# Laying out the blocks of a triangular inverse with VectorE's 32x32 turns in place of transfers through DRAM

## The chip, the cores and the metric

The kernel runs on one core of a Trainium2 chip. The metric is device time in microseconds (us): the median over several runs, beside one more execution that was profiled.

The core's engines each work through their own instructions in program order: TensorE (PE, whose weight loads stand apart as PEld), VectorE (DVE), ScalarE (ACT), GpSimd (POOL) and SyncE (SP), which here issues almost all transfers. An instruction that waits holds up everything behind it on its engine.

## The reference

One step of a decoder layer for 256 prompt tokens and 8 x 8 sample tokens (320 in all, width 2048). A single projection `w_in` feeds two branches, a gated delta rule (32 heads of 128 x 128 state) and a sparse attention; both are projected, merged by gates and projected again. The change lies in the delta rule alone:

```python
a_strict = jnp.where(strict, einsum('bhnid,bhnjd->bhnij', kb, k) * decay, 0.0)
rhs = concatenate([v * beta[..., None], kb * exp(G)[..., None]], axis=-1)
sol = lax.linalg.triangular_solve(a_strict, rhs, left_side=True, lower=True, unit_diagonal=True)
```

The kernel solves this by forming the inverse of each unit triangular 128 x 128 matrix: its four 32 x 32 diagonal blocks are inverted first, and the rest follows from products of blocks.

## The kernel before

**The main stream.** `stream` walks over weight units of 1024 x 128 (512 KB). For each, SP loads `raw`, ACT rounds it to `whi`, DVE forms the rest `wlo = raw - whi`, and PE runs 24 matmuls of 128 x 320 (`xh` and `xl` by `whi`, `xh` by `wlo`). ACT's and DVE's share of a unit is emitted up to two units ahead of PE (`split_ahead`, `lead=2`), in three buffers each.

**Side work.** Everything else is written as generators (`kq_gen`, `inverse`, `prompt_chain`, `sample_chain`, `norm_gen` and others). After the sixth k of a unit and after its end, `side_round` lets each generator emit its next piece, if its inputs are ready by the planner's clock (`Clock`, which adds a price for every instruction). `spawn(..., first=True)` puts a generator ahead of the others. So the prices decide where in each engine's program a piece stands; on the chip only the order and the semaphores count.

**The recurrent stage** runs from about 850 us to 1660 us, in eight groups of four heads, one group for every 24 units of the stream. For a group, `kq_gen` forms twelve matrices in `BT` (128 x 12 x 128: four heads by two prompt chunks, and four for the samples). `inverse` turns them into `XT`, and `prompt_chain`, `sample_chain` and `norm_gen` go on from there. `norm_gen` sends a small power (`sc<-sc,mh`, 128 x 6) to POOL, and ACT's scaling of `ot` waits for it. There is one buffer each of `BT`, `blk`/`X` and `XT`.

**`inverse` before the change** (called from `kq_gen` once both head pairs of a group stand in `BT`):

1. Seven transfers write `BT`'s diagonal and off-diagonal blocks to DRAM (`d_b`, `d_o`); one reads the 48 diagonal blocks back into `blk`, one block to a partition.
2. POOL inverts all 48 together: 31 steps of a product (`tmpx`) and a subtraction (`X`), on 48 partitions.
3. POOL copies the result turned (`blk<-X`); two transfers write both forms to DRAM (`d_x`), and fifteen read blocks into `XT`, `blk` and `X` with rows on partitions.
4. PE multiplies blocks in four places: 16 products of 32 x 32 (`ps<-X,blk`), 28 more (`XT`, `blk`), 8 of 64 x 64 and 8 more. ACT brings each result from PSUM into `blk`, `X` or `XT`.

All transfers are issued by SP, in the queue that also carries the weights: 25 for a group, 200 in all.

## Time and profile before

| | |
|---|---|
| time, median of 3 runs (2125.87 to 2126.71) | 2125.89 us |
| time of the profiled execution | 2128.34 us |
| its span | 2126.6 us |
| granted TensorE clock | 0.998 |
| busy in the span: PE / DVE / ACT / POOL | 2093.1 / 1416.3 / 985.3 / 464.0 us |
| recurrent stage, 960 to 1660 us: PE / DVE / ACT / POOL | 698.4 / 522.1 / 396.8 / 313.4 us |

The span is the time from the first to the last instruction of the profiled execution; the launch around it adds 1.7 us. A row of the timeline has start, duration, engine, instruction, what it writes and reads, shapes and how many alike were merged; in brackets stands the idle time ahead of it and what ended it. All instructions are recorded by one helper, so they all carry one line number, and are told apart by the tiles that they write and read.

### The profile page before, as it was taken

The page shows a single profiled execution, that of the slowest core. Times are in us where ns is not written, and L with a number is a line of the kernel's source. Part 1 is how long each engine was busy: PE and PEld are TensorE (multiplying, and loading weights), DVE is VectorE, ACT ScalarE, POOL GpSimd, SP SyncE. Part 2 cuts the span into 40 slices and gives each one's busy share as a digit, 9 for nine tenths or more (in the row PEclk, how much of TensorE's full clock was granted, in tenths as well). Part 3 has the DMA queues.
Part 4 walks back from the last instruction along what each step waited for, and adds up shares of the span by engine and source line. Part 5 has one row for each costly group of instructions (what it writes and reads, how often), then busy time and mean ns, then how long its engine had stood idle before and what let it go on. Part 6 is the DMA issues. An engine that isn't in the chain of part 4 may idle for free.

```text
span 2126.6 us, 45305 instructions
## 1 busy us (share of the span) xinstructions
PE 2093.1 (98%) x17769; PEld 2020.2 (95%) x17769; DVE 1416.3 (67%) x2898; ACT 985.3 (46%) x2253; POOL 464.0 (22%) x661
## 2 busy tenths in 40 slices
PE   7999999999999999999999999999999999999997
PEld 7999989999999999899999999999999999999997
DVE  4776647889855477777878786868665545455543
ACT  3224473333344455465646464656545534333343
POOL 1001000000010108361818181818080000000000
PEclk9999999999999999999999999999999999999999
DMA  9996659776578667686868686868687867555562
GB/s 344 333 337 184 177 140 261 224 210 197 167 239 247 202 186 203 160 233 181 228 173 232 173 232 171 234 170 229 171 245 214 247 204 211 169 154 150 163 181 81
DMA packets 713989, 438.99 MB, mean 206 GB/s; under 512 B 73936, under 2 KB 697136, under 8 KB 711472
## 3 DMA queue, kind: packets, MB, share of 16 engines
q1 hardware_dynamic: 709696, 413.45, 68.3%
q0 software_dynamic: 3616, 21.02, 3.0%
q8 instruction: 139, 2.28, 0.5%
q10 hardware_dynamic: 464, 1.65, 0.2%
q14 instruction: 74, 0.61, 0.1%
HBM read 386.81 MB, written 48.94 MB: 205 GB/s over the span
## 4 chain that ended last, share of the span: by engine, by line
PE 70%; issue 22%; DVE 3%; DMA 2%; ACT 2%; SPq 0%; DVEq 0%; POOL 0%; POOLq 0%; ACTq 0%
PE pm L64 54%; PE ps L64 16%; DVE S L64 1%; DVE wlo L64 1%; DMA rawx<-in_w_ada_dram 1%; DMA a<-in_w_ada_dram 1%; DMA out_dram<-s 0%; DVE ps L64 0%; ACT whi L64 0%; DMA qiS<-d_qi 0%; ACT ot L64 0%; SPq L64 0%; DMA c<-in_c_sample_dram 0%; ACT s L64 0%; DMA cst<-in_state_conv_dram 0%
## 5 line engine op out<-in xcount | busy, mean ns | idle before, releaser
L64 PE MATMUL pm<-xh,whi 128*128 128x320 f32 (+1 forms) x3108 | 942.5, 317 | 2.7 <-DVE qiS L64 1.3
L64 PE MATMUL pm<-xl,whi 128*128 128x320 f32 (+1 forms) x3108 | 910.2, 307 | 0.3 <-DVE xl L64 0.2
L64 DVE TENSOR_TENSOR wlo<-raw,whi 128x1024 fp32r<-128x1024 f32 x466 | 576.8, 1247 | 245.8 <-ACT whi L64 233.7
L64 PEld LDWEIGHTS pm<-xh,whi 128*128 128x128 f32 x3108 | 584.2, 188 | 27.9 <-issue 20.2
L64 PEld LDWEIGHTS pm<-xl,whi 128*128 128x128 f32 x3108 | 585.0, 188 | 1.6 <-DVE xl L64 0.7
L64 ACT ACTIVATE whi<-raw 128x1024 fp32r<-128x1024 f32 x466 | 488.5, 1058 | 168.1 <-PE pm L64 103.8
L64 PE MATMUL pm<-xh,wlo 128*128 128x320 f32 (+1 forms) x3108 | 521.3, 307 | 0.5 <-DVE wlo L64 0.5
L64 PEld LDWEIGHTS pm<-xh,wlo 128*128 128x128 f32 x3108 | 469.4, 188 | 0.9 <-DVE wlo L64 0.9
L64 POOL TENSOR_TENSOR X<-X,tmpx 48x31 f32<-48x31 f32 (+15 forms) x248 | 175.5, 708 | 19.4
L64 POOL TENSOR_TENSOR tmpx<-blk,X 48x31 f32<-48x31 f32 (+15 forms) x248 | 162.0, 653 | 53.0 <-DMA blk<-d_b 34.8
L64 DVE SCALAR_TENSOR_TENSOR ps<-xp,cs,ps 128x344 f32<-128x344 f32 x192 | 111.5, 581 | 6.8
L64 POOL TENSOR_TENSOR sc<-sc,mh 128x6 f32<-128x6 f32 (+1 forms) x24 | 44.3, 1848 | 285.4 <-DVE sc L64 206.0
L64 PE MATMUL pm<-y1h,whi 128*128 128x320 f32 x336 | 99.5, 309 | 1.8 <-DVE M L64 0.9
L64 POOL TENSOR_TENSOR rfin<-rfin,mh 128x3 f32<-128x3 f32 x1 | 0.8, 848 | 455.5 <-DVE rfin L64 455.5
L64 PE MATMUL pm<-y1l,whi 128*128 128x320 f32 x336 | 99.1, 307 | 0.0
L64 DVE SCALAR_TENSOR_TENSOR S<-S,gtr,ps 128x128 f32<-128x128 f32 x256 | 67.4, 342 | 0.1
L64 PEld LDWEIGHTS pm<-y1h,whi 128*128 128x128 f32 x336 | 62.8, 187 | 2.3 <-ACT whi L64 2.3
L64 PE MATMUL ps<-xh,whi 128*128 128x320 f32 (+1 forms) x220 | 64.7, 309 | 0.0
L64 ACT ACTIVATE xp<-pm 128x256 f32<-128x256 f32 (+1 forms) x128 | 32.0, 304 | 70.5 <-PE pm L64 70.5
L64 ACT ACTIVATE ot<-ot,sc 128x128 f32<-128x128 f32 x96 | 29.9, 390 | 73.5 <-DVE sc L64 73.5
L64 PE MATMUL ps<-xl,whi 128*128 128x320 f32 (+1 forms) x220 | 63.7, 304 | 0.0
L64 PEld LDWEIGHTS pm<-y1l,whi 128*128 128x128 f32 x336 | 63.1, 188 | 0.0
(403 smaller groups left out, 2793.3 us busy)
## 6 DMA issues: line engine op xcount, KB each, us to landing
raw<-in_w_in_dram SPq DMA_DIRECT2D x328, 512.0 KB
raw<-in_w_pa_dram SPq DMA_DIRECT2D x64, 512.0 KB
rawx<-in_w_ada_dram SPq DMA_DIRECT2D x18, 1024.0 KB
a<-in_w_ada_dram SPq DMA_DIRECT2D x16, 1024.0 KB
S<-in_state_gdn_dram SPq DMA_DIRECT2D x32, 512.0 KB
out_dram<-S SPq DMA_DIRECT2D x32, 512.0 KB
raw<-in_w_pb_dram SPq DMA_DIRECT2D x32, 512.0 KB
raw<-in_w_out_dram SPq DMA_DIRECT2D x32, 512.0 KB
```

What stands on the lines that cost most here:

```text
L64: made = fn(*args, **kw)
```

## The change

The blocks stay in SBUF. ACT and POOL copy the 48 diagonal blocks of `BT` side by side into `X` (block k of a matrix stays on partitions 32k to 32k+31), and one DVE instruction turns all 32 x 32 squares, so that each partition holds one whole block; 80 of the 128 partitions then carry filler. POOL's 31 steps are the same with 128 partitions. Two more DVE turns bring the inverse back in both forms, and ACT and POOL copy blocks into place. The off-diagonal blocks go by copies into two new tiles, `BO` and `BD`. All 25 transfers of a group and their DRAM tiles are gone. `inverse` is spawned ahead of the other side work.

To make room, the mask is built a second time in `gdn_open` (`select`) instead of being kept, and the tiles `sc` shrink from 56 to 44 columns by letting `qf` and one of the tail factors use columns that are free by then.

```diff
-        self.tmp = a.tile([48, 256], F32, name="tmpx")
+        self.tmp = a.tile([128, 256], F32, name="tmpx")
+        self.BO = a.tile([128, 4, 64], F32, name="BO")
+        self.BD = a.tile([128, 8, 32], F32, name="BD")
...
-            self.spawn(self.inverse(h // 2, G))
+            self.spawn(self.inverse(h // 2, G), first=True)
...
+    def blocks(self, out, in_):
+        self.emitted += 1
+        self.nc.vector.transpose(out, in_)
...
-        for k in range(4):
-            nc.sync.dma_start(d_b[k].rearrange("m j i -> j m i"), BT[32 * k:32 * k + 32, :, 32 * k:32 * k + 32])
-        nc.sync.dma_start(d_o[:, :, 0:64], BT[0:64, 0:8, 64:128])
+        stage = X.rearrange("p (m i) -> p m i", i=32)
+        nc.gpsimd.memset(X[:, 384:1024], 0.0)
+        for k, s in enumerate(quarters):
+            if k % 2:
+                self.act(stage[s, 0:12, :], BT[s, :, s])
+            else:
+                nc.gpsimd.tensor_copy(stage[s, 0:12, :], BT[s, :, s])
+        BO, BD = self.BO, self.BD
+        self.act(BO[64:128], BT[0:64, 4:8, 64:128])
         for o in (0, 64):
-            nc.sync.dma_start(d_o[o // 2:o // 2 + 32, :, 64:96], BT[o:o + 32, 0:8, o + 32:o + 64])
+            self.act(BD[o:o + 32], BT[o:o + 32, 0:8, o + 32:o + 64])
+        nc.gpsimd.tensor_copy(BO[0:64], BT[0:64, 0:4, 64:128])
         self.BT.put(BT)
+        yield self.ready(X)
+        self.blocks(blk.rearrange("p (j i) -> p i j", i=32), X.rearrange("p (m i) -> p i m", i=32))
+        nc.gpsimd.memset(X, 0.0)
+        nc.gpsimd.memset(X[:, 0:1024:33], 1.0)
         yield
...
-        nc.gpsimd.tensor_copy(blk[0:48].rearrange("p (c i) -> p c i", i=32), X.rearrange("p i c -> p c i"))
         yield
...
-        nc.sync.dma_start(d_x[0].rearrange("k m i c -> (k m) (i c)"), Xt[0:48])
-        nc.sync.dma_start(d_x[1].rearrange("k m i c -> (k m) (i c)"), blk[0:48])
...
+        self.blocks(blk.rearrange("p (m i) -> p i m", i=32), X.rearrange("p (i c) -> p i c", c=32))
+        cols = X.rearrange("p (i c) -> p c i", c=32)
+        self.blocks(cols, cols)
...
+        for k, s in enumerate(quarters):
+            if k % 2:
+                self.act(XT[s, :, s], DT[s])
+            else:
+                nc.gpsimd.tensor_copy(XT[s, :, s], DT[s])
...
+        for o in (0, 32):
+            self.act(XE[o + 64:o + 96, :, o:o + 32], DN[o:o + 32, 4:8, :])
+            self.act(XE[o:o + 32, :, o:o + 32], DT[o + 64:o + 96, 4:8, :])
```

Three places in the program show what moves. The first is **POOL**, between the last step of one group's inverse and the first step of the next (`sc` of 128 x 10 belongs to `kq_gen`, of 128 x 6 to `norm_gen`). Before:

```order
L64 TENSOR_TENSOR X<-X,tmpx 48x31
L64 COPY blk<-X 48x1024
L64 TENSOR_TENSOR sc_8004<-sc_8004,mh 128x10
L64 MEMSET X 32x8x32
L64 MEMSET X 32x4x32 x2
L64 MEMSET X 48x1024
L64 MEMSET X 48x32
L64 TENSOR_TENSOR sc_8002<-sc_8002,mh 128x6
L64 TENSOR_TENSOR tmpx<-blk,X 48x31
```

And in the changed kernel, between two groups:

```order
L64 TENSOR_TENSOR X<-X,tmpx 128x31
L64 MEMSET X 32x4x32 x3
L64 COPY X<-X 32x4x32 x2
L64 COPY XT_7982<-blk 32x12x32 x2
L64 TENSOR_TENSOR sc_7999<-sc_7999,mh 128x10
L64 TENSOR_TENSOR sc_7998<-sc_7998,mh 128x6
L64 MEMSET X 128x640
L64 COPY X<-BT_7973 32x384 x2
L64 COPY BO<-BT_7973 64x256
L64 MEMSET X 128x1024
L64 MEMSET X 128x32
L64 TENSOR_TENSOR sc_8001<-sc_8001,mh 128x6
```

The turned copy is gone; seven copies, with a memset of 640 columns, have come, and the power of one `norm_gen` now stands behind them, and behind a memset of `X` that has to wait for DVE's first turn.

The second is **DVE**, where the two turns behind POOL's last step stand among the weights' `wlo`, in the changed kernel:

```order
L64 TENSOR_TENSOR wlo_82<-raw_75,whi_79 128x1024
L64 TENSOR_SCALAR sc_7998<-sc_7998 128x10
L64 TENSOR_TENSOR wlo_83<-raw_75,whi_80 128x1024
L64 STREAM_TRANSPOSE blk<-X 128x32x32
L64 STREAM_TRANSPOSE X<-X 128x32x32
L64 SCALAR_TENSOR_TENSOR zf_7967<-cth_7948,zf_7967 128x320
L64 TENSOR_TENSOR wlo_81<-raw_76,whi_78 128x1024
```

Before, DVE had nothing of the inverse there; now the `wlo` behind the turns waits until POOL is through.

The third is **ACT**, where the products of blocks come back from PSUM. Before, two pieces with a `whi` between:

```order
L64 ACTIVATE blk<-ps_70 32x256 x2
L64 ACTIVATE whi_79<-raw_75 128x1024
L64 ACTIVATE X<-ps_72 32x4x32 x2
L64 ACTIVATE X<-ps_67 32x4x32
L64 ACTIVATE XT_7986<-ps_72 32x8x32 x2
L64 ACTIVATE whi_80<-raw_75 128x1024
```

In the changed kernel:

```order
L64 ACTIVATE whi_80<-raw_77 128x1024
L64 ACTIVATE XT_7982<-blk 32x12x32 x2
L64 ACTIVATE X<-ps_67 32x4x32 x2
L64 ACTIVATE X<-ps_69 32x4x32
L64 ACTIVATE XT_7982<-ps_67 32x8x32 x2
L64 ACTIVATE X<-X 32x4x32
L64 ACTIVATE X<-blk 32x4x32
L64 ACTIVATE X<-X 32x4x32
L64 ACTIVATE X<-blk 32x4x32
L64 ACTIVATE whi_78<-raw_77 128x1024
```

Six copies have joined the five that were there, ahead of the same `whi`.

## The prediction

> **What bounds the kernel now.** I read the page's head first, then the busy time by stage, then single places.

> ```profile
> span 2126.6 us, 45305 instructions
> PE 2093.1 (98%) x17769; PEld 2020.2 (95%) x17769; DVE 1416.3 (67%) x2898; ACT 985.3 (46%) x2253; POOL 464.0 (22%) x661
> PE   7999999999999999999999999999999999999997
> ```

> PE is busy 98% of the span, and in all slices but the first and the last. The next view gives the three stretches that the change can reach: entry, body and what follows.

> ```profile
> 850.00:960.00 110.00, 107.96 (x880) 103.14 (x879) 82.37 (x198) 64.87 (x189) 55.08 (x78) 1.00 0.74 194
> 960.00:1660.00 700.00, 698.36 (x5755) 668.99 (x5755) 522.05 (x1230) 396.84 (x1076) 313.40 (x431) 1.00 0.75 204
> 1660.00:2115.00 455.00, 452.92 (x3105) 451.98 (x3103) 221.75 (x295) 169.65 (x250) 0.41 (x1) 1.00 0.59 172
> ```

> The columns after the length are PE, PEld, DVE, ACT, POOL, the granted clock, the DMA share and GB/s. PE stands idle for 2.04, 1.64 and 2.08 us in them: **5.8 us in all is what any change to the other engines could win here.** But a busy PE need not be at its peak, so its pace is looked at, in the timeline around one of the inverse's products:

> ```profile
> 1182.05 0.31 PE L64 MATMUL pm<-xh,whi 128*128 128x320 f32 x1
> 1182.20 0.30 PE L64 MATMUL pm<-xl,whi 128*128 128x320 f32 x1
> 1182.34 1.33 PE L64 MATMUL pm<-xh,wlo 128*128 128x320 f32 x8
> 1183.61 0.69 PE L64 MATMUL ps<-X,blk 32*32 32x32 f32 x32
> 1184.23 0.41 PE L64 MATMUL pm<-xh,whi 128*128 128x320 f32 x1
> 1184.48 0.30 PE L64 MATMUL pm<-xl,whi 128*128 128x320 f32 x1
> ...
> 1128.83 0.49 PE L64 MATMUL ps<-ident,ot 128*128 128x128 f32 x3
> 1129.08 0.39 PE L64 MATMUL pm<-xh,whi 128*128 128x320 f32 x1
> ```

> The main matmuls start every 0.147 us (1182.05, 1182.20, 1182.34), before and after a side product, and the 32 small ones follow within 0.1 us (eight from 1182.34 end their slots at 1183.52). So PE is issuing all the time; the inverse is inserted work, not something that PE waits for. In the waits of 960 to 1660 us there is indeed no row of PE for `blk`, `X` or `XT`; those that concern the stream's operands are:

> ```profile
> DVE wlo L64 <- ACT whi L64: 64.0, 38, 3.5
> ACT ot L64 <- DVE sc L64: 63.3, 13, 6.1
> ACT whi L64 <- PE pm L64: 13.0, 16, 1.9
> PEld pm L64 <- ACT whi L64: 2.8, 3, 1.2
> PE pm L64 <- ACT whi L64: 2.1, 3, 0.9
> ```

> No `whi` waits for a weight's transfer there. PE's few waits are for `whi`, and ACT's largest is for `sc`, which comes from POOL by way of DVE.

> **The change part by part.**

> *PE's work.* Each group keeps its products: 16 and 28 of 32 x 32, 8 and 8 of 64 x 64, with the same rows and columns of the array, only from other tiles. What differs is where they stand. Counted in the two programs, small work interrupts the stream at 323 places before and 311 after. Does an interruption cost something by itself? The three transposes above start at 1128.83 and the stream goes on at 1129.08, 0.25 us for three; the first main matmul of the other piece takes 0.25 us to the next instead of 0.147, and 0.09 us lay ahead. At the dearest 12 x 0.19 = 2.3 us are won, at the cheapest nothing, if these parts only begin and finish the small ones' own work, as the three transposes suggest. I take 0.

> *The transfers.* 200 leave SP's queue:

> ```profile
> DMA packets 713989, 438.99 MB, mean 206 GB/s; under 512 B 73936, under 2 KB 697136, under 8 KB 711472
> ```

> Most of the 73,936 small packets are theirs, rows of 32 numbers. Since `whi` doesn't wait for weights in this stage, this wins nothing: it is hidden already. What is late next is POOL.

> *What is added.* The prices come from these groups and single rows:

> ```profile
> L64 DVE STREAM_TRANSPOSE a<-a 128x1024 f32<-128x1024 f32 x24 | 28.6, 1222 | 0.0
> L64 POOL COPY blk<-X 48x1024 f32<-48x1024 f32 x8 | 18.7, 2336 | 0.5
> L64 POOL MEMSET X<- 48x1024 f32 x8 | 7.6, 952 | 148.8 <-PE ps L64 81.7 <-DMA d_z<-zf 44.8 <-DMA raw<-in_w_in_dram 22.4
> L64 POOL MEMSET XT<- 128x1536 f32 x1 | 1.4, 1385 | 0.5 <-DMA d_z<-t 0.5
> L64 POOL TENSOR_TENSOR X<-X,tmpx 48x31 f32<-48x31 f32 (+15 forms) x248 | 175.5, 708 | 19.4
> L64 POOL TENSOR_TENSOR tmpx<-blk,X 48x31 f32<-48x31 f32 (+15 forms) x248 | 162.0, 653 | 53.0 <-DMA blk<-d_b 34.8
> L64 ACT ACTIVATE xp<-pm 128x256 f32<-128x256 f32 x64 | 24.4, 381 | 70.5 <-PE pm L64 70.5
> L64 ACT ACTIVATE cth<-ps 128x344 f32<-128x344 f32 x64 | 29.0, 453 | 43.9 <-DVE ps L64 43.8
> L64 ACT ACTIVATE X<-ps 32x128 f32<-32x128 f32 x24 | 6.4, 268 | 5.6 <-PE ps L64 5.2
> ```

> - DVE: 3 turns of 1.22 us, 3.7 us for a group. That row reads along the columns, the new ones in steps of 128 bytes, which no DVE row shows. Bounds: 1.22 us, and 2.45 times that (3.0 us) by the ratio of POOL's turned copy to its memset (2336 to 952 ns). I take 1.22, the row of the same instruction.
> - ACT: four copies of 384 columns (0.48 each, between 0.381 and 0.453 and a little on), three of 256 (0.38), four of 128 (0.27): 1.92 + 1.14 + 1.08 = 4.1 us for a group.
> - POOL: copies at 0.93 to 2.28 ns a column (memset, turned copy), and I take the dearer: four of 384, one of 256, two of 128 make 2048 columns, 4.7 us; the memset of 640 adds 0.6 and the turned copy takes 2.3 away: 3.0 us more for a group.
> - The 31 steps cost 337.5 / 8 = 42.2 us for a group, on 48 partitions. With 128? From below the same: the memsets give 0.93 ns a column on 48 partitions and 0.90 on 128. From above 128/48 times, 112 us, if two-input steps went by partitions; no row shows one that wide. I take the same, because the only pair of rows says so.

> Over 107 us, a group's period (24 units), DVE goes from 75% to 78%, ACT from 57% to 61%, POOL from 45% to 48%. None is full, so on the average it is all beside PE.

> *Is the inverse in time?* In the changed order its first product stands at least 17 units (of 24 x 0.147 = 3.53 us) behind the last product that feeds `BT`, 60 us plus the small work between, some 65 us at the least. It needs six `BT` products on DVE (6 x 0.34), copies (2), a turn, the memset (1.0), 42.2 us with 62 gaps of 0.08 as the timeline shows them, and two turns: 2.1 + 2 + 1.2 + 1.0 + 47 + 2.4 = 56 us. With turns at 3.0 us it is 61, still in time. PE doesn't wait at the products.

> *Queues.* Where the two turns stand, all of DVE's later work waits for POOL's last step. But DVE prepares up to two units ahead, 7 us; a wait of some us there uses up lead, not PE's time. The tender place is another:

> ```profile
> 1121.08 1.87 ACT L64 ACTIVATE ot<-ot,sc 128x128 f32<-128x128 f32 x6 [5.37 <-DVE sc L64]
> 1127.84 1.99 ACT L64 ACTIVATE whi<-raw 128x1024 fp32r<-128x1024 f32 x2
> 1129.21 2.26 POOL L64 TENSOR_TENSOR sc<-sc,mh 128x6 f32<-128x6 f32 x1 [1.02 <-DVE sc L64]
> 1131.44 0.62 POOL L64 TENSOR_TENSOR tmpx<-blk,X 48x247 f32<-48x247 f32 x1
> ```

> ACT stood 5.37 us for `sc`, which had waited in POOL's queue behind steps of the inverse; afterwards it caught up, and of the pair of `whi` from 1127.84 the first was done near 1128.9, for a PE unit that starts at 1129.08. **The margin is about 0.2 us.** There are 16 such places, two for a group. The change moves POOL's chain against them, in each group otherwise. If a place becomes up to 1 us earlier or later, evenly, it loses on the mean (0.8 x 0.8 / 2) / 2 = 0.16 us beyond its 0.2 of margin: 16 x 0.16 = 2.6 us. Of PE's 2.1 us of waits for `whi` now, I let 0.5 go.

> [...] These rows show DVE and POOL in each other's way:

> ```profile
> 1134.33 0.62 POOL L64 TENSOR_TENSOR tmpx<-blk,X 48x255 f32<-48x255 f32 x1
> 1134.80 1.24 DVE L64 TENSOR_TENSOR wlo<-raw,whi 128x1024 fp32r<-128x1024 f32 x1
> 1135.03 1.55 POOL L64 TENSOR_TENSOR X<-X,tmpx 48x255 f32<-48x255 f32 x1
> ```

> The step at 1135.03 takes 1.55 us where most take 0.7: it stood until `wlo` was through. [...]

> **The sum.** PE's work 0, waits at the products 0, waits for `whi` +2.6 - 0.5 = +2.1 us. On the profiled execution that makes 2128.34 + 2.1; it stands 2.45 us above the median of the runs, so against the median 2125.89 + 2.1 = **2128.0 us**, within what a measurement can tell from no change (0.2%, 4.25 us).

> **The rivals.**

> 1. *Slower: the powers come late out of POOL.* The changed order puts memsets and copies, and in some groups DVE's first turn, ahead of `norm_gen`'s power. For it: 3.0 us more in that queue for a group, and margins of 0.2 us. Against it: the generators are paced, and chains now start earlier. It decides from 0.5 us of lateness at each of the 16 places on: 16 x 0.3 = 4.8 us, 2130.7; with 1 us, 16 x 0.8 = 12.8 us, 2138.7.
> 2. *Faster: the waits go.* Without transfers the chain starts earlier, and the powers may fall between chains. All 5.8 us of idle time gone gives 2120.1; under 2121.6 it counts as faster. Nearly every wait would have to vanish, though 2.1 us lie behind the stage.
> 3. *It doesn't do what it says:* the steps get dearer with the partitions, 112 us instead of 42.2, more than a group's period; the inverse would come some 60 us late in each group, about +500 us. The memsets speak against it.

> **Chances.** The forecast (within 4.25 us) 0.66; rival 1, 0.27; rival 2, 0.06; rival 3, 0.01. The range leaves out rival 3, rival 2's far end and the last of rival 1: 2121 to 2138. So faster by over 0.2% has 0.06, within it 0.66, slower 0.28.

> **What would show it.** Right: PE idle near 4 us over the three stretches, turns near 1.22 us, POOL's steps at the same mean, no PE wait for the inverse's tiles, DMA share lower in the stage with no effect on PE. Rival 1: rows of PE waiting for `whi` or `wlo` several times as large, each some us behind a late `sc`. Rival 3: steps of over 1 us at the mean. What would upset all this is a wait that no row shows now, above all DVE's turns holding a `wlo` for longer than its lead.

## The result and the profile after

| | before | after |
|---|---|---|
| median (range) | 2125.90 us (2125.87 to 2126.71) | 2155.39 us (2152.14 to 2156.28) |
| ratio, 95% interval | | 1.0135 (1.0117 to 1.0153) |
| profiled execution: time / span | 2128.34 / 2126.6 us | 2155.66 / 2154.0 us |
| mean granted clock | 0.998 | 0.994 |

The kernel became 29.5 us slower; 2128.0 had been forecast, with 2138 as the upper end. The head of the page of the changed kernel, and its packets:

```profile
span 2154.0 us, 45150 instructions
PE 2103.4 (98%) x17769; PEld 2026.9 (94%) x17769; DVE 1461.9 (68%) x2921; ACT 1023.8 (48%) x2341; POOL 492.9 (23%) x720
DMA packets 658436, 426.65 MB, mean 198 GB/s; under 512 B 19536, under 2 KB 642736, under 8 KB 655920
```

54,400 of the packets under 512 bytes are gone, PE runs as many matmuls, and its share of 98% looks as before. The same three stretches, columns as in the prediction:

```profile
850.00:960.00 110.00, 104.00 (x860) 97.68 (x859) 87.03 (x201) 63.34 (x183) 54.98 (x83) 0.98 0.58 160
960.00:1660.00 700.00, 685.62 (x5585) 654.72 (x5585) 546.51 (x1236) 418.55 (x1132) 333.46 (x471) 0.99 0.67 185
1660.00:2115.00 455.00, 453.90 (x3106) 453.50 (x3105) 226.39 (x301) 175.40 (x259) 1.32 (x1) 1.00 0.63 183
```

PE stands idle for 6.00, 14.38 and 1.10 us, 21.5 in all where it was 5.8. Behind the stage nothing is lost. In the first two stretches the granted clock is no longer 1.00. PE's largest waits from 850 to 1700 us (total, times, longest):

```profile
PE ps L64 <- DVE X L64: 8.9, 5, 2.9
PE pm L64 <- ACT whi L64: 6.1, 6, 1.5
PE pm L64 <- DVE wlo L64: 4.1, 5, 1.8
```

The first row is the wait that the prediction had ruled out: the inverse's first product (`ps<-X,BD`) waits for DVE's turn into `X`. The groups of the turns (busy, mean ns), the old ones of `a` for comparison:

```profile
L64 DVE STREAM_TRANSPOSE blk<-X 128x1024 f32<-128x1024 f32 x16 | 34.0, 2127 | 8.2 <-POOL X L64 8.2
L64 DVE STREAM_TRANSPOSE a<-a 128x1024 f32<-128x1024 f32 x24 | 28.6, 1223 | 0.0
L64 DVE STREAM_TRANSPOSE X<-X 128x1024 f32<-128x1024 f32 x8 | 17.0, 2121 | 0.3
```

The turns in steps of 128 bytes take 2.12 us, 1.74 times the contiguous one. What that does is seen in the timeline, first on DVE and then on PE, at the dearest place:

```profile
1505.08 2.00 DVE L64 STREAM_TRANSPOSE blk<-X 128x1024 f32<-128x1024 f32 x1 [3.01 <-POOL X L64]
1507.12 2.01 DVE L64 STREAM_TRANSPOSE X<-X 128x1024 f32<-128x1024 f32 x1
```

```profile
1509.27 0.74 PE L64 MATMUL ps<-X,BD 32*32 32x32 f32 x32 [2.92 <-DVE X L64]
1509.94 0.64 PE L64 MATMUL pm<-xh,whi 128*128 128x320 f32 x1
1510.37 0.47 PE L64 MATMUL pm<-xl,whi 128*128 128x320 f32 x1
1510.64 0.47 PE L64 MATMUL pm<-xh,whi 128*128 128x320 f32 x1
1510.91 0.47 PE L64 MATMUL pm<-xl,whi 128*128 128x320 f32 x1
```

PE waits 2.92 us, and afterwards the main matmuls start every 0.27 us (1510.37, 1510.64, 1510.91) in place of 0.147: for a while the clock is halved (granted clock 0.50 from 1509.79 to 1513.20 us). The clock's records put half clock into five slots of 3.41 us in the stage (from 854.4, 1025.1, 1175.3, 1509.8 and 1615.6 us), and into none there before the change. Windows cut along these slots show PE's busy time, then the granted clock:

```profile
851.02:854.43 3.41, 1.75 (x41) 1.00 0.00 0
854.43:857.85 3.42, 3.42 (x15) 0.50 0.61 168
1021.68:1025.10 3.42, 1.58 (x11) 1.00 0.39 109
1025.10:1028.51 3.41, 3.41 (x16) 0.50 0.83 213
...
1567.82:1571.23 3.41, 1.88 (x14) 1.00 1.00 265
1571.23:1574.64 3.41, 3.41 (x25) 1.00 0.76 205
```

The slots in which PE was busy for 1.75 and 1.58 us are followed by one at half clock; after 1.88 us the clock stays. At half clock a matmul takes 0.27 us (1510.37 to 1510.91 for two) in place of 0.147, so a slot costs 3.41 x (1 - 0.147 / 0.27) = 1.55 us, and five cost 7.8.

**Where the time went:** 15.7 us more idle time and 7.8 us at half clock make 23.5 of the span's 27.4 us; the other 4 us aren't placed.

### The profile page after: what moved, and what is told of

It is laid out like the page before. It is cut to its first block, busy times and chain, and to the rows that moved or that the text cites. A ratio compares the mean times of both kernels' runs of the same rounds, so it can differ in the third digit from the quotient of the medians.

```text
span 2154.0 us, 45150 instructions
## 1 busy us (share of the span) xinstructions
PE 2103.4 (98%) x17769; PEld 2026.9 (94%) x17769; DVE 1461.9 (68%) x2921; ACT 1023.8 (48%) x2341; POOL 492.9 (23%) x720
## 2 busy tenths in 40 slices
PE   7999999999999999999999999999999999999997
## 3 DMA queue, kind: packets, MB, share of 16 engines
q8 instruction: 139, 2.28, 0.4%
## 4 chain that ended last, share of the span: by engine, by line
PE 52%; issue 24%; DVE 9%; POOL 8%; DMA 3%; ACT 3%; SPq 1%; DVEq 0%; POOLq 0%; ACTq 0%
PE pm L64 38%; PE ps L64 14%; POOL X L64 4%; POOL tmpx L64 4%; DVE wlo L64 2%; DVE blk L64 1%; DVE S L64 1%; DVE ps L64 1%; DMA raw<-in_w_ada_dram 1%; SPq L64 1%; ACT whi L64 1%; ACT ot L64 1%; DMA rawx<-in_w_ada_dram 1%; DMA a<-in_w_ada_dram 1%; DVE X L64 0%
## 5 line engine op out<-in xcount | busy, mean ns | idle before, releaser
L64 PE MATMUL pm<-xh,whi 128*128 128x320 f32 (+1 forms) x3108 | 945.2, 318 | 8.1 <-ACT whi L64 6.1
L64 PE MATMUL pm<-xl,whi 128*128 128x320 f32 (+1 forms) x3108 | 913.4, 308 | 0.4 <-DVE xl L64 0.3
L64 DVE TENSOR_TENSOR wlo<-raw,whi 128x1024 fp32r<-128x1024 f32 x466 | 577.8, 1247 | 232.0 <-ACT whi L64 221.9
L64 PEld LDWEIGHTS pm<-xh,whi 128*128 128x128 f32 x3108 | 587.2, 189 | 33.8 <-issue 18.9
L64 PEld LDWEIGHTS pm<-xl,whi 128*128 128x128 f32 x3108 | 587.9, 189 | 1.6 <-DVE xl L64 0.8
L64 ACT ACTIVATE whi<-raw 128x1024 fp32r<-128x1024 f32 x466 | 489.4, 1058 | 178.9 <-PE pm L64 113.6
L64 PE MATMUL pm<-xh,wlo 128*128 128x320 f32 (+1 forms) x3108 | 524.7, 309 | 4.6 <-DVE wlo L64 4.6
L64 PEld LDWEIGHTS pm<-xh,wlo 128*128 128x128 f32 x3108 | 471.6, 189 | 6.9 <-DVE wlo L64 6.8
L64 POOL TENSOR_TENSOR X<-X,tmpx 128x31 f32<-128x31 f32 (+15 forms) x248 | 177.8, 717 | 19.4
L64 POOL TENSOR_TENSOR tmpx<-blk,X 128x31 f32<-128x31 f32 (+15 forms) x248 | 170.9, 689 | 18.6
L64 DVE SCALAR_TENSOR_TENSOR ps<-xp,cs,ps 128x344 f32<-128x344 f32 x192 | 111.5, 581 | 6.8
L64 POOL TENSOR_TENSOR rfin<-rfin,mh 128x3 f32<-128x3 f32 x1 | 0.8, 850 | 471.9 <-DVE rfin L64 471.9
L64 PE MATMUL pm<-y1h,whi 128*128 128x320 f32 x336 | 99.4, 308 | 0.0
L64 PE MATMUL pm<-y1l,whi 128*128 128x320 f32 x336 | 99.1, 307 | 0.0
L64 POOL TENSOR_TENSOR sc<-sc,mh 128x6 f32<-128x6 f32 (+1 forms) x24 | 41.3, 1719 | 236.4 <-DVE sc L64 164.4
L64 ACT ACTIVATE xp<-pm 128x256 f32<-128x256 f32 (+1 forms) x128 | 32.0, 304 | 76.0 <-PE pm L64 76.0
L64 DVE SCALAR_TENSOR_TENSOR S<-S,gtr,ps 128x128 f32<-128x128 f32 x256 | 67.5, 344 | 0.1
L64 PE MATMUL ps<-xh,whi 128*128 128x320 f32 (+1 forms) x220 | 64.7, 309 | 0.0
L64 ACT ACTIVATE ot<-ot,sc 128x128 f32<-128x128 f32 x96 | 29.9, 390 | 71.9 <-DVE sc L64 71.9
L64 PE MATMUL ps<-xl,whi 128*128 128x320 f32 (+1 forms) x220 | 63.7, 304 | 0.0
L64 PEld LDWEIGHTS pm<-y1l,whi 128*128 128x128 f32 x336 | 63.1, 188 | 0.0
L64 PEld LDWEIGHTS pm<-y1h,whi 128*128 128x128 f32 x336 | 62.8, 187 | 0.0
```

Of the source, the lines that this page charges most:

```text
L64: made = fn(*args, **kw)
```

## The experiments

My theory was: *the turns' steps make them long, the long turns come late for PE, and the longest of those waits halve the clock.* The rivals: *the place* (the planner's price of 1.245 us for a turn puts the products too early, and only that is wrong), and *the order* (any new order of the program, or late powers, whatever a turn takes). Results, in the order of the runs; each ratio is to the kernel before on the same chip, and the last column counts the slots at half clock in the profiled execution between 840 and 2120 us.

| kernel | median us | ratio (95%) | half-clock slots |
|---|---|---|---|
| changed kernel | 2155.39 | 1.0135 (1.0117 to 1.0153) | 5 |
| e1_flat: all turns contiguous | 2135.13 | 1.0038 (1.0025 to 1.0051) | 0 |
| e1_sides: first turn reads in steps only | 2155.07 (one run) | | 5 |
| e2_price: turn priced at 2.1 us | 2160.94 | 1.0164 (1.0138 to 1.0189) | 6 |
| e3_last: inverse spawned last | 2148.05 | 1.0095 (1.0076 to 1.0114) | 4 |
| e5_swap: product waits for one turn | 2137.79 | 1.0057 (1.0040 to 1.0074) | 1 |
| e6_t1: and the first turn contiguous | 2135.73 | 1.0043 (1.0026 to 1.0059) | 0 |
| e7_last: e6_t1, inverse last | 2135.69 | 1.0043 (1.0026 to 1.0059) | 1 |
| e8_norm: e7_last, scaling later | 2138.02 | 1.0063 (1.0046 to 1.0080) | 3 |
| e9_norm1: e6_t1, scaling later | 2136.59 | 1.0058 (1.0041 to 1.0075) | 1 |
| e10_norm: before, scaling later | 2134.71 | 1.0046 (1.0029 to 1.0063) | 2 |
| e4_first: before, inverse first | 2135.15 | 1.0051 (1.0032 to 1.0070) | 1 |
| e11_bpow: before, price of the power | 2128.11 | 1.0001 (0.9991 to 1.0010) | 0 |
| e12_bdve: before, price of DVE | 2133.65 | 1.0029 (1.0019 to 1.0038) | 0 |
| e13_spow: e6_t1, price of the power | 2139.87 | 1.0051 (1.0036 to 1.0066) | 2 |
| e14_sdve: e6_t1, price of DVE | 2147.25 | 1.0091 (1.0072 to 1.0110) | 1 |

### The turns' length alone

```diff
-        self.blocks(blk.rearrange("p (j i) -> p i j", i=32), X.rearrange("p (m i) -> p i m", i=32))
+        self.blocks(blk.rearrange("p (i c) -> p i c", c=32), X.rearrange("p (i c) -> p i c", c=32))
...
-        self.blocks(blk.rearrange("p (m i) -> p i m", i=32), X.rearrange("p (i c) -> p i c", c=32))
+        self.blocks(blk.rearrange("p (i c) -> p i c", c=32), X.rearrange("p (i c) -> p i c", c=32))
...
-        self.blocks(cols, cols)
+        self.blocks(X.rearrange("p (i c) -> p i c", c=32), X.rearrange("p (i c) -> p i c", c=32))
```

> The changed kernel with its three turns reading and writing along the columns (contiguous, as the turns of before did); every engine's order stays as in the changed kernel. It leaves out the right layout of the blocks, so the numbers in the inverse are others; the work is the same. Theory 1 (the turns are long because of their steps of 128 bytes, and come late for PE): a turn falls from 2.09 to about 1.25 us, PE's waits at the products (9.7 us) fall under 2, the half-clock windows go from five to none or one, and the time is 2132 to 2140 us. Theory 3 (the new order as such, the powers late out of POOL, whatever a turn takes): the products may come in time, but the whi and wlo waits stay (11 us) and with them some of the half-clock windows; 2146 or more.

This kernel leaves out the right layout of the blocks. The planner prices both forms alike, and on DVE, ACT and POOL the order of the rows in the trace is the changed kernel's, row by row. The groups of the turns, and PE's waits from 850 to 1700 us, in e1_flat:

```profile
L64 DVE STREAM_TRANSPOSE blk<-X 128x1024 f32<-128x1024 f32 x16 | 19.8, 1239 | 7.3 <-POOL X L64 7.3
L64 DVE STREAM_TRANSPOSE X<-X 128x1024 f32<-128x1024 f32 x8 | 10.0, 1246 | 0.3
```

```profile
PE pm L64 <- ACT whi L64: 6.0, 7, 1.3
PE ps L64 <- DVE X L64: 1.8, 2, 1.4
PE pm L64 <- DVE wlo L64: 1.3, 2, 0.9
```

0.88 us less for a turn takes 7.1 us from the product waits, 2.8 from `wlo`'s and every slot at half clock: 1.0135 falls to 1.0038. **About 20 of the 29 us are the turns' length**, shown with the order kept. The turns now also take what the planner prices (1.245 us), so this run doesn't part "long" from "longer than priced". The `whi` waits stay. Of the 8 us that e1_flat still loses, 7.4 are idle time of PE in the first two stretches (11.0 us against 3.7 before).

In e1_sides the first line alone is changed, to write contiguously while it reads in steps:

> The changed kernel with the first turn writing contiguously and still reading in steps of 128 bytes; the second writes in steps alone, the third reads and writes in steps, as they were. It leaves out the right layout. If the write's stride alone costs, the first turn takes about 1.25 us and the other two stay at 2.0 to 2.1; if the read's stride costs too, the first stays near 2.0. The time: under theory 1 somewhat below the changed kernel (one of a group's three turns shorter: 2148 to 2155), under theory 3 the same as the changed kernel.

These two rows of its timeline, at the places of two first turns:

```profile
886.46 1.96 DVE L64 STREAM_TRANSPOSE blk<-X 128x1024 f32<-128x1024 f32 x1
1021.83 2.03 DVE L64 STREAM_TRANSPOSE blk<-X 128x1024 f32<-128x1024 f32 x1
```

Reading in steps costs by itself nearly all (1.96 and 2.03 us); so does writing (the turn at 1505.08 above writes in steps and reads contiguously, 2.00). The time stayed that of the changed kernel, though it is a single run.

### The place of the products

```diff
+            if op == "transpose" and len(outs[0].shape) == 3:
+                return 2.1
```

> The changed kernel with its work untouched, but the planner's price of a turn in steps put at 2.1 us in place of 1.245, so that the products that wait for turns are emitted later. Theory 2 (only the place of the products in PE's order is at fault, since the planner took the turns too short): turns stay at 2.09 us, the product waits (9.7 us) fall under 3, the half-clock windows fall from five to one or two, 2136 to 2144 us. Theory 1 in its strict form (long turns hold DVE's queue and so wlo, wherever the products stand): wlo and whi waits stay at 11 us or grow; 2146 to 2152. Theory 3: 2150 or more.

PE's waits from 850 to 1700 us in e2_price, with the last row further down:

```profile
PE pm L64 <- ACT whi L64: 11.4, 8, 3.2
PE pm L64 <- DVE wlo L64: 8.0, 7, 1.8
...
PE ps L64 <- DVE X L64: 0.6, 1, 0.6
```

The products are now nearly in time, as that rival said, and yet the kernel is slower: `wlo` and `whi` wait longer. At 1135.19 us, for one, PE stands 1.84 us for a `wlo` that DVE could only begin behind a first turn of 2.16 us. The true price alone doesn't mend it: the turns are still long in DVE's queue, and the new order has bad places of its own. As "only the price is wrong" the rival falls. But the true price also moved the rows, and the order rival had asked for 2150 or more here, so this run doesn't say what late products cost by themselves; e5_swap says more of that.

### The first turn of two, and the turn ahead of `wlo`

e5_swap needs the right layout with fewer steps. The turn in steps now gives the form that the first product reads, and the other form is the contiguous turn of that:

```diff
-        self.blocks(blk.rearrange("p (m i) -> p i m", i=32), X.rearrange("p (i c) -> p i c", c=32))
-        cols = X.rearrange("p (i c) -> p c i", c=32)
-        self.blocks(cols, cols)
+        blk, X = X, blk
+        self.blocks(X.rearrange("p (m c) -> p c m", c=32), blk.rearrange("p (i c) -> p c i", c=32))
+        self.blocks(blk.rearrange("p (m i) -> p m i", i=32), X.rearrange("p (m c) -> p m c", c=32))
```

> The changed kernel, with the right layout, but the two turns behind the inverse rearranged: the one in steps of 128 bytes now gives the form that the first product reads, and the other form is made from it by a contiguous turn. So the first product waits for one turn of about 2.1 us and not for two (4.2 us), and the pair takes 3.3 us; the turn ahead of POOL's steps stays in steps. The order moves by a few rows only. If the long turns act through the products' lateness: the product waits (9.7 us) fall under 2, the half-clock windows behind them (four of five) go, the wlo waits (4.6 us) and the window at about 1025 us stay: 2155.4 - 9.7 - 4 x 1.7 = 2139, 2135 to 2143. If they act through DVE's queue alone (wlo held behind turns): one turn of a group shorter by 0.9 us, 2150 or more. If the order is at fault: 2150 or more.

PE's waits for these operands in e5_swap (the tiles' names are exchanged, so the product waits for `blk`):

```profile
PE pm L64 <- ACT whi L64: 5.0, 4, 1.5
PE pm L64 <- DVE wlo L64: 2.8, 3, 1.8
PE ps L64 <- DVE blk L64: 0.9, 1, 0.9
```

2137.8 against 2139: nearly all of the wait at the products goes, with its four slots, though two of a group's three turns are still long; the long `wlo` wait stays. So most of the turns' cost came through the late products. That the number fits so closely is in part luck: the half-clock slot at the `wlo` wait went too, and another came at 903 us. The windows along the slots show both:

```profile
1015.96:1019.38 3.42, 2.31 (x16) 2.05 (x14) 3.38 (x4) 2.90 (x8) 0.29 (x1) 1.00 0.77 223
1019.38:1022.79 3.41, 2.69 (x19) 2.68 (x20) 3.33 (x9) 1.06 (x1) 1.86 (x3) 1.00 0.40 108
899.91:903.32 3.41, 1.48 (x21) 0.83 (x14) 3.41 (x9) 0.00 (x0) 3.12 (x4) 1.00 1.03 275
903.32:906.74 3.42, 3.42 (x16) 3.42 (x14) 3.38 (x14) 3.03 (x10) 3.08 (x5) 0.50 1.07 282
```

This 1.8 us wait lies across the edge of two slots, PE is busy for 2.31 and 2.69 us of them, and the clock stays; behind a slot with 1.48 us of PE busy it is halved, at 903 us.

e6_t1 makes the first turn contiguous as well, and lets copies and POOL step instead:

```diff
-        stage = X.rearrange("p (m i) -> p m i", i=32)
-        nc.gpsimd.memset(X[:, 384:1024], 0.0)
+        stage = X.rearrange("p (i m) -> p m i", m=32)
+        nc.gpsimd.memset(X.rearrange("p (i m) -> p i m", m=32)[:, :, 12:32], 0.0)
...
-        self.blocks(blk.rearrange("p (j i) -> p i j", i=32), X.rearrange("p (m i) -> p i m", i=32))
+        self.blocks(blk.rearrange("p (i j) -> p i j", j=32), X.rearrange("p (i m) -> p i m", m=32))
...
-        B = blk.rearrange("p (j i) -> p j i", i=32)
+        B = blk.rearrange("p (i j) -> p j i", j=32)
```

> The kernel of e5_swap with the first turn contiguous too: ACT's and POOL's copies write the blocks of X in steps, and POOL's 31 steps read blk in steps of 128 bytes. Two of a group's three turns are then contiguous. If the first turn's 2.1 us ahead of wlo make the wlo waits: they fall from 4.6 to about 2, the last half-clock window goes, 2131 to 2136 us, and the trace looks like that of e1_flat. If POOL's products tmpx take longer for the steps (0.69 to 1.0 us), a group's chain is 10 us longer and the products wait again: 2145 or more. Theory 3 (order): no change against e5_swap.

It gave 2135.7, with `wlo` waits of 1.9 us and no slot at half clock, as expected; against e5_swap that is within the intervals. So a kernel with the right layout loses no more than e1_flat.

### The order

e3_last drops `first=True`; e7_last does so on e6_t1, in nearly the order of e3_last.

> The changed kernel with the inverse spawned behind the other side work, as it was before the change, and no other edit; the order moves on all engines. Theory 3 (putting the inverse ahead of the rest delays the powers): the whi waits fall from 7 to 3 us and the time to 2140 to 2147 us. Theories 1 and 2: the turns are as long and as wrongly priced as before, so waits at the products remain; 2148 to 2160.

> The kernel of e6_t1 with the inverse spawned behind the other side work, so nearly the order of e3_last (2148.1 us) with two of three turns contiguous. If the turns' length is the cause in that order as well: of e3_last's waits those for X (about 6 us) and wlo (5.6 us) and three half-clock windows (5 us) go, and the wait for a transfer of a state (3.5 us) stays: 2129 to 2136. If in that order something else made the waits: 2143 or more.

Spawning the inverse first goes with a loss where the turns are long (1.0135 against 1.0095) and with none where they are short (1.0043 twice). In e3_last's order too, short turns win 0.5%, 11 us.

What remained, 8 to 9 us, looked like the first rival of the prediction: `whi` behind ACT's wait for `sc`. Three kernels let the scaling of `ot` stand later, and e4_first, a kernel of before, spawns the inverse first (it and e10_norm take `PT` ahead of the wait for a PSUM bank, which leaves the order as it is):

```diff
         self.tt(m[:, 12:18], m[:, 6:12], self.mh.to_broadcast([128, 6]), OP.pow, eng=nc.gpsimd)
-        yield
+        yield self.ready(m) + 2.0
```

> The kernel of e7_last (2135.7 us), with ACT's scaling of ot emitted at least 2 us of the planner's clock behind the power that it needs, so that a whi stands ahead of it and ACT waits less for sc. Its whi waits of 1.64 and 1.16 us come each right behind such a wait. If the late powers are what is left (the first rival of the prediction): the whi waits (2.7 us) go, ACT's wait for sc (about 70 us over 16 places) falls by more than a third, 2131 to 2134 us. If what is left is spread over waits of all kinds that any new order brings: 2134 to 2140, with waits at other places.

> The kernel of e6_t1 (2135.7 us, inverse spawned ahead of the others) with the same later scaling of ot. Its whi waits are larger (5.9 us, five waits). If they come from the late powers: 2129 to 2133 us. If the order's chances decide: anywhere from 2132 to 2142, with waits at other places.

> The kernel before, with the same later scaling of ot (and PT taken before the wait for a PSUM bank, as in the changed kernel, which the planner then needs). Only 2 us of its waits are for whi, so at most 2 us are to be won: 2122 to 2126 if the late powers made them; if a new order by itself brings waits, 2126 to 2134.

> The kernel before, with its transfers, but the inverse spawned ahead of the other side work (and PT taken before the wait for a PSUM bank). If spawning it first is itself harmful (theory 3): 2130 to 2136, with whi and wlo waits as in the changed kernel. If it isn't: within 4 us of before, and no half-clock window.

The later scaling helps nowhere, but it hardly did what it was for: ACT's wait for `sc` fell by a tenth at most (from 70.0 to 62.8 us in e8_norm, from 62.9 to 56.2 in e9_norm1, from 73.5 to 70.3 in e10_norm), where e8_norm's expectation had asked for more than a third. PE's waits for `whi` went from 2.7 to 7.7 us in e8_norm and stayed at 5.9 in e9_norm1. So these kernels don't decide whether late powers make the rest. And two kernels with all the old transfers, e10_norm and e4_first, lose 10 and 11 us. e4_first lands where its expectation put a first spawn that is harmful by itself, with 6.6 us of waits for `whi`; with short turns the same move cost nothing. PE's waits from 850 to 1700 us in e10_norm:

```profile
PE pm L64 <- ACT whi L64: 5.9, 5, 3.1
PE ps L64 <- DMA cst<-in_conv_w_dram: 2.2, 2, 1.4
```

So a new order by itself can cost what was left. Is it all of it? Two kernels of before and two of e6_t1 with a small change of one price (the power 1.3 us for 1.6, or DVE's fixed part 0.15 for 0.16) were to tell:

> The kernel before, with its work and transfers untouched; only the planner's price of POOL's power is 1.3 us (as measured) in place of 1.6, which moves rows in the order. (PT is taken before the wait for a bank, which by itself leaves the order as it was.) If the order of before is an unusually good one, and any other loses by chance what the short turns still lose: 2130 to 2138 us on a chip where before takes 2126. If a new order costs nothing of itself: within 4 us of before.

> The kernel before, with the planner's fixed price of a VectorE instruction at 0.15 us in place of 0.16: a smaller change of a price, which moves more rows. The same two cases as for e11_bpow: 2130 to 2138 us, or within 4 us of before.

> The kernel of e6_t1 (two of three turns contiguous) with the planner's price of POOL's power at 1.3 us. If what is left of the loss is the chance of the order: as for the orders of before, 2130 to 2138, and now and then as good as before. If the added copies and turns cost something in any order: above both e11_bpow and e12_bdve by 4 us or more.

> The kernel of e6_t1 with the planner's fixed price of a VectorE instruction at 0.15 us. The same two cases as for e13_spow.

By the case named ahead of them, the added work costs something in any order: e13_spow and e14_sdve lie 6 and 14 us above the dearer of the two kernels of before (4 us had been asked for), and both above the 2130 to 2138 us of the chance case. All orders together are less clear. Four new orders of the old work give 1.0001 to 1.0051, mean 1.0032; seven orders with short turns (e1_flat, e6_t1 to e9_norm1, e13_spow, e14_sdve) give 1.0038 to 1.0091, mean 1.0055. The ranges overlap, and with the same price changed the short turns lie 0.5% and 0.6% higher. **Shown is that order alone can cost up to 11 us, and that in the changed kernel's order 20 are the turns' length. Open is how much of the last 8 to 9 us is the added work:** the means suggest 0.2%, some 5 us, but so few orders don't prove it. The order of before was met by one other order only (e11_bpow). No kernel here beat the kernel before.

## Why the prediction was wrong

*What held.* PE still bounds the kernel. The transfers were hidden: no kernel here is faster without them (54,400 small packets less, the DMA share in the stage 0.67 for 0.75). The partitions cost next to nothing, by the groups of POOL's steps in the changed kernel:

```profile
L64 POOL TENSOR_TENSOR X<-X,tmpx 128x31 f32<-128x31 f32 (+15 forms) x248 | 177.8, 717 | 19.4
L64 POOL TENSOR_TENSOR tmpx<-blk,X 128x31 f32<-128x31 f32 (+15 forms) x248 | 170.9, 689 | 18.6
```

348.7 / 8 = 43.6 us for a group against the 42.2 taken, so the third rival is out. That PE's own work is unchanged was not isolated; the 4 us that aren't placed could lie there.

*The first step that failed: a turn at 1.22 us.* It took 2.12. The bounds (1.22 to 3.0) held it, but I took the row of the same instruction though its access was another. That row goes along the columns (1.22 us); the new turns go in steps of 32 elements and take 2.12 us at the mean, 1.74 times as long. Why steps cost this much no run here isolates.

*The second, and the heavier one: "PE doesn't wait at the products".* It rested on 56 us of need against 65 in the order, with room even for turns at 3.0 us; it put this wait at 0, and 8.9 us were measured. The need was too small and the room misread. The need, in the group of 1505 us: `BT` was complete at 1436.3, and the chain on POOL went

```profile
1440.21 0.64 POOL L64 MEMSET X<- 128x640 f32 x1
1440.78 1.06 POOL L64 COPY X<-BT 32x384 f32<-32x384 f32 x2
1441.90 0.39 POOL L64 COPY BO<-BT 64x256 f32<-64x256 f32 x1
1452.73 1.17 POOL L64 MEMSET X<- 128x1024 f32 x2 [10.44 <-DVE blk L64]
1453.97 0.24 POOL L64 TENSOR_TENSOR tmpx<-blk,X 128x31 f32<-128x31 f32 x1
```

POOL stood 10.44 us until the first turn was through, which came up in DVE's queue only at 1450.36; I had priced that wait at nothing. From `BT` to the product at 1509.27 went 73 us. And the order had no fixed room: the planner emits a product when its own clock says that the turns are done, so 65 us was a least distance and no slack. The product stands right behind the turns, and a turn that takes 0.87 us longer than its price makes it late by as much, twice: 1.7 us. PE waited in five of the eight groups, 0.4 to 2.9 us and 1.8 at the mean.

*The third: "a wait of some us there uses up lead, not PE's time".* DVE in the changed kernel, and PE:

```profile
1021.28 2.16 DVE L64 STREAM_TRANSPOSE blk<-X 128x1024 f32<-128x1024 f32 x1
1023.35 2.31 DVE L64 TENSOR_TENSOR wlo<-raw,whi 128x1024 fp32r<-128x1024 f32 x2
```

```profile
1024.58 2.08 PE L64 MATMUL pm<-xh,wlo 128*128 128x320 f32 x8 [1.84 <-DVE wlo L64]
```

The turn waited for nothing here and still cost PE 1.84 us. At this place DVE had no lead left, since it had worked without a gap for 8 us ahead of the turn; the two units are an upper bound. The last sentence of the prediction, a `wlo` held longer than its lead, names it, but no chance was given to it.

*The fourth: the half clock was no term at all.* In the trace of before nothing in the stage shows it (granted clock 1.00 in all three stretches); 7.8 us of the loss are its, as estimated above. No slot ahead of the five was wholly idle: PE was busy in them for 1.75, 1.58, 2.06, 0.52 and 1.41 us of 3.41.

*Smaller terms.* By the heads of the two pages, ACT got 38.5 / 8 = 4.8 us of work more for a group (4.1 forecast), POOL 28.9 / 8 = 3.6 (3.0). Waits for `whi` went from 2.1 to 6.1 us, twice the 2.1 us that were forecast, and late `sc` stands ahead of some of them (ACT stands 5.47 us for it until 1156.96, and PE 1.11 us for the next `whi`), so the first rival was partly real. It can't have made the 20 us that go with the turns' length. The 8 to 9 us that are left lie within its price (4.8 to 12.8 us), and whether they are its stays open, since no kernel here took the wait for `sc` away. POOL's copies cost less than taken where nothing holds them. This view of a tile gives shortest, median and longest:

```profile
L64 POOL COPY X<-BT x16: 495/502/1427, 790.2 to 1548.8; 32x384 f32<-32x384 f32 x16
```

0.50 us at the median against 0.88 taken. The two longest (1.43 us from 877.87, 1.42 from 1547.32) ran beside a `wlo` (877.72 to 878.94, 1547.17 to 1548.38) and ended 0.36 us behind it; the other fourteen took at most 0.53 us. That is like the step at 1135.03 in the prediction, which stood until `wlo` was through. While a turn runs POOL mostly waits; the one POOL instruction beside a turn in the changed kernel, a power of 128 x 10 at 1295.47, took its usual 1.96 us.

## What to carry to other kernels

Price an instruction by a row with the same access, not only the same operation and shape (here 2.12 us for a turn in steps against 1.22 along the columns); where a planner orders the program, look up what price it has for it, because the excess over that price can arrive in full at whoever is emitted right behind. In a stream that is 98% busy, slack must be read place by place, and a single wait can cost more than its length: here the one of 1.84 us at 1024.58 was followed by a slot at half clock, by the estimate above 1.55 us more, so it cost nearly twice its length. A change that moves the order has to be compared with other orders of the old kernel too: here reordering alone cost between nothing and 11 us.

## What the hardware showed unexpectedly

```profile
1171.87:1175.29 3.42, 2.06 (x92) 1.00 0.04 13
1175.29:1178.70 3.41, 3.41 (x34) 0.50 0.09 11
...
1612.19:1615.60 3.41, 1.41 (x38) 1.00 0.00 0
1615.60:1619.02 3.42, 3.42 (x15) 0.50 0.58 155
```

- POOL's two-input steps took nearly the same on 48 and on 128 partitions (0.68 us at the mean before, 0.70 in the changed kernel), and reading `blk` in steps of 128 bytes left them so (0.71 in e6_t1). In e6_t1 one product waits, for 1.1 us; in e5_swap one did for 0.9.
